# A hybrid convolution and attention block on eight cores: statistics kept per quad, a shorter lead in the output projection, a new order and new first loads

## The chip, the cores and the metric

One Trainium2 chip, eight cores in two dies (cores 0 to 3 and 4 to 7). Each core computes one of eight sequences with the same program and without talking to the others. The metric is the device time of the slowest core, in microseconds. A second, slower state hits some executions of most of these kernels: the cores of one die, sometimes of both, show a lower granted TensorE clock. Only fast runs are compared.

In the views, PE is TensorE (matrix multiplication; PEld are its weight loads), DVE is VectorE, ACT ScalarE, POOL GpSimd, and SP SyncE, which here only issues transfers (DMA). SBUF is the on-chip memory that the program plans by hand; PSUM is the one that matmuls write, used here in eight banks. A table load is an operation that ScalarE's records show between some functions, such as Ln and Silu: 1.28 us each in these traces (mean of 17 on core 2 of the kernel before).

## The reference, cut to what matters

```python
h = rms_norm(x, ln1_g)                         # x: 2048 x 2048 per core
c_val, c_gate, q, k, v = split(h @ w_in)       # 1024 columns each
y = c_val * sigmoid(c_gate)
y = causal_depthwise(y, 31 taps) + b_dw
y_conv = silu(layer_norm over the 1024 channels of y)
y_attn = chunked attention, 8 heads of 128 (band of 9 chunks of 64)
y = concat(rms_norm(y_conv), rms_norm(y_attn))
x = x + y @ w_out                              # called W_out below
h2 = rms_norm(x, ln2_g)
x = x + relu(h2 @ w_ff1)**2 @ w_ff2            # 2048 -> 8192 -> 2048
```

## The kernel before

The program lists its operations once; a scheduler of its own then gives every operation a modelled duration and picks, for each engine, an order that is fixed when the program is built. At run time each engine works through its list and waits where an input is late. So a constant of that model moves instructions without any change to what is computed.

```python
XLAT = 180.0; DMA_LAT = 2200.0; DMA_BPNS = 230.0           # ns, ns, bytes per ns
# GpSimd: 150 + 1.7 n;  DMA issue: 1000 (GpSimd), 60 (SyncE)
# DVE: (n / fast + 130) / .96, transposes as plain copies
```

The tokens are cut into 16 tiles of 128 and four quads of 512; the convolution channels into eight groups. The stages, in order: V (norm of x, transposes, V projection), eight heads of attention, eight conv groups, W_out, feed-forward. The conv groups keep statistics of quad 0 only; those of the other quads are computed inside W_out:

```python
for cc in range(6):                   # groups 0..5
    conv_load(cc + 1)
    for qd in range(4): conv_gate(cc, qd)
    conv_dw(cc)                       # depthwise: 64 small matmuls, all 4 quads
    stat(0, cc, cc == 0)              # Square (ScalarE), ones-matmul, sum on GpSimd
...
for qd in range(4):                   # groups 6 and 7: all gates, then depthwise
    conv_gate(6, qd); conv_gate(7, qd)
for cc in (6, 7):
    conv_dw(cc); stat(0, cc, False)
...
def out_attn(t):                      # attention half of W_out, tile t
    ... 8 transposes of on -> yT ...
    for cb in range(4):
        ... 8 matmuls yT x wo[0] ...
        stt(xx, ps(b), ra[:, t], xx, mult, add)   # VectorE: x += ra * psum
def out_conv(t):                      # conv half, then write out, then the row norm
    ... 4 x (8 matmuls, stt) ...
    P.dma("sp", ..., out_d[t], xs[t % 3])
    norm_tile(...)                    # Square, Ln, Exp (ScalarE), scale (VectorE), 16 transposes
...
fin_stats(0)
for t in range(3): out_attn(t)
for c in range(8): fin_cc(0, c)       # normalise, Silu, Square
fin_end(0)
for t in range(NT):
    out_conv(t)
    if t + 3 < NT:
        loadx2(t + 3)                 # into xs[t % 3], which out_conv(t) has just used
        out_attn(t + 3)
    ... statistics and fin_cc of quad t // 4 + 1 ...
```

Of the kernel before, what the change touches and what calls it, by code (L numbers as in the profile page):

```python
# [22 lines left out]
DMA_LAT = 2200.0  # L23
DMA_BPNS = 230.0
# [22 lines left out]
class Prog:  # L47
# [127 lines left out]
    def _ew(self, eng, fn, r, w, fast=1.0):  # L175
        n = max(self.n(x) for x in w)
        if eng == "dve":
            d = (n / fast + 130) / .96
        else:
            d = 150 + n * 1.7  # L180
        self.op(eng, fn, r, w, d)
# [13 lines left out]
    def ts(self, out, in0, s1, op0, s2=None, op1=None, eng="dve"):  # L195
        r = [in0] + [s for s in (s1, s2) if s is not None and not isinstance(s, float)]
        kw = {} if op1 is None else {"op1": op1}
        self._ew(eng, lambda e: e.tensor_scalar(out=out, in0=in0, scalar1=s1, scalar2=s2, op0=op0, **kw), r, [out])

    def vtr(self, out, in_):  # L200
        self._ew("dve", lambda e: e.transpose(out=out, in_=in_), [in_], [out])
# [10 lines left out]
    def dma(self, eng, key, out, in_, r=(), w=()):  # L212
        r = list(r)
        w = list(w)
        nb = 0
        for x, l in ((in_, r), (out, w)):
            if x.tensor.__class__.__name__.startswith("SB"):
                l.append(x)
                nb = max(nb, self.n(x) * 128 * 4)
        self.op(eng, lambda e: e.dma_start(out=out, in_=in_), r, w, 1000.0 if eng == "pool" else 60.0, dma=True, key=key, nbytes=nb)  # L220
# [167 lines left out]
def build_program():  # L388
# [40 lines left out]
    identf = const("identf", [128], F32)  # L429
    identb = const("identb", [128], BF16)  # L430
    onesf = const("onesf", [128], F32)
    onesb = const("onesb", [128], BF16)
    pv = const("pv", [NPV], F32)
    rk = [const(f"rk{i}", [16], F32) for i in range(2)]
    st1 = const("st1", [16, 2], F32)
    r1 = const("r1", [16], F32)
    st2 = const("st2", [16, 2], F32)
    r2 = const("r2", [16], F32)
    ssa = const("ssa", [16, 8], F32)
    ra = const("ra", [16], F32)  # L440
    rat = const("rat", [16], F32)
    rc = const("rc", [16], F32)
    rct = const("rct", [16], F32)
    rz = const("rz", [16, 1], F32)
    kst = const("kst", [4, 4], F32)
    assert D0 + 53504 <= top[0], (top[0] - D0)
# [18 lines left out]
    P.dma("sp", "id", identf[:, :], id_d)  # L465
# [6 lines left out]

    loadx(0)
    P.dma("sp", "pv", pv[:, :], pv_d)
    P.dma("sp", "g", g1[:, :], bass.AP(gv_d.tensor, 0, [[0, 128], [1, 2048]]))
    for q in range(2):
        P.dma("pool", f"wv0{q}", wv[:, 0, 8 * q:8 * q + 8, :], wv_d[0][:, 8 * q:8 * q + 8, :])
    loadx(1)
    loadx(2)
    for q in range(2):  # L480
        P.dma("pool", f"wv1{q}", wv[:, 1, 8 * q:8 * q + 8, :], wv_d[1][:, 8 * q:8 * q + 8, :])
    copy(identb[:, :], identf[:, :])
# [3 lines left out]
    P.memset(onesf[:, :], 1.0, "dve")  # L486
    P.memset(onesb[:, :], 1.0, "dve")
    P.memset(V[:, :, :, 128:130], 1.0, "pool")
# [16 lines left out]
    for t in range(NT):  # L505
# [6 lines left out]
        norm_tile(xs1[t % 3][:, :], t, st1, r1, g1[:, :], hb[t % 2], dst, (4 + 2 * (t % 2), 5 + 2 * (t % 2)))  # L512
        if t + 3 < NT:
            loadx(t + 3)
        for hf in range(2):
# [10 lines left out]
    EB = [sb(f"EB{i}", [640], BF16, D0 + 1280 * i) for i in range(8)]  # L526
    ef = [sb(f"ef{i}", [256], F32, D0 + 10240 + 1024 * i) for i in range(2)]
    eB = [sb(f"eB{i}", [256], F32, D0 + 12288 + 1024 * i) for i in range(2)]
    gA = sb("gA", [1024], F32, D0 + 14336)
    oj = [sb(f"oj{i}", [128], BF16, D0 + 18432 + 256 * i) for i in range(2)]  # L530
# [3 lines left out]
    def proj(h):  # L534
        hp = h % 2
        for which in (0, 1):
            s = nw[0] % 3
            nw[0] += 1
            P.dma("pool", f"wqk{s}", wqk[s][:, :, :], wqk_d[h, which])
# [71 lines left out]
    P.dma("sp", "g", gA[:, :], bass.AP(gv_d.tensor, 2 * 2048, [[0, 128], [1, 1024]]))  # L611
# [12 lines left out]
    wc = [sb("wc0", [2, 16, 128], BF16, D0 + 24 * KB), sb("wc1", [2, 16, 128], BF16, B + 56 * KB)]  # L624
    pad = sb("pad", [32, 2, 128], BF16, D0)
    raw = sb("raw", [32, 2, 32], BF16, D0 + 16 * KB)
    cs = [sb(f"cs{i}", [512], BF16, D0 + 38 * KB + 8448 + 4096 + 1024 * i) for i in range(2)]
    G = [sb(f"G{i}", [512], BF16, D0 + 32 * KB + 1024 * i) for i in range(2)]
    th = [sb(f"th{i}", [512], F32, D0 + 34 * KB + 2048 * i) for i in range(2)]
    Gt = [sb(f"Gt{i}", [32, 66], BF16, D0 + 38 * KB + 4224 * i) for i in range(2)]  # L630
    ysum = [sb(f"ysum{i}", [512], F32, D0 + 38 * KB + 8448 + 2048 * i) for i in range(2)]
    nv = [0]
    ng = [0]
# [4 lines left out]
    def conv_gate(cc, qd):  # L638
# [4 lines left out]
        bb = []  # L643
        for which in (1, 0):
            b = nv[0] % 3
            nv[0] += 1
            bb.append(b)
            for k in range(16):
                mm(ps(b), w[:, which, k, :], hT[:, qd, k, :], k == 0, k == 15)
            if which == 1:  # L650
                i = ng[0] % 2
                act(th[i][:, :], ps(b), AF.Tanh, scale=0.5)
        stt(G[i][:, :], th[i][:, :], 1.0, ps(bb[1]), ALU.add, ALU.mult)
        ng[0] += 1
        o_ = bass.AP(gt, 1 + 16 * qd, [[32 * 66, 128], [1, 16], [66, 32]])
        P.vtr(o_, G[i][:, :].rearrange("p (b i) -> p b i", i=32))

    def conv_dw(cc):
        s = SLOT[cc]
        gt = Gt[cc % 2]  # L660
        P.dma("pool", "raw", raw[:, :, :, :], toep_d[cc])
        if cc == 0:
            P.memset(pad[:, 0:16, :, :], 0.0)
            P.memset(pad[:, 16:32, :, :], 0.0)
        for ih in range(2):
            for q in range(4):
                P.copy(pad[32 * q:32 * q + 32, 16 * ih:16 * ih + 16, :, 32 * q:32 * q + 32], raw[32 * q:32 * q + 32, 16 * ih:16 * ih + 16, :, :], eng="pool")
        for i in range(32):
            b = 3 + i // 8
            o_ = ps(b, (i % 8) * 64, (i % 8) * 64 + 64)  # L670
            mm(o_, pad[:, i, 0, :], gt[:, i, 1:65], True, False)
            mm(o_, pad[:, i, 1, :], gt[:, i, 0:64], False, True)
        for qd in range(4):
            P.vtr(y[:, s, qd, :].rearrange("p (b i) -> p b i", i=32), bass.AP(psf, 3 * 512 + 16 * qd, [[4096, 128], [1, 16], [64, 32]]))

    def stat(qd, cc, first):
        s = SLOT[cc]
        yy = y[:, s, qd, :]
        su = ysum[qd % 2][:, :]
        if first:  # L680
            P.ts(su, yy, pc(54), ALU.add, eng="pool")
        else:
            tt(su, yy, su, ALU.add, eng="pool")
        c = cs[cc % 2]
        act(c[:, :], yy, AF.Square, scale=0.5, bias=pc(bdw + cc))
        mm(ps(7), onesb[:, :], c[:, :], first, cc == 7)


    h2b = sb("h2b", [2048], BF16, D0 + 32 * KB)
    yT = sb("yT", [8, 128], BF16, D0 + 36 * KB)  # L690
    mu = sb("mu", [512], F32, D0 + 38 * KB)
    rs = sb("rs", [512], F32, D0 + 40 * KB)
    sl = [sb(f"sl{i}", [512], F32, D0 + 42 * KB + 2048 * i) for i in range(2)]

    def fin_stats(qd):
        su = ysum[qd % 2][:, :]
        v2 = sl[0][:, :]

        act(rs[:, :], ps(7), AF.Identity, scale=1.0 / 1024)
        mm(ps(7), onesf[:, :], su, True, True)  # L700
        act(mu[:, :], ps(7), AF.Identity, scale=1.0 / 1024)
        tt(v2, mu[:, :], mu[:, :], ALU.mult)
        stt(rs[:, :], v2, -0.25, rs[:, :], ALU.mult, ALU.add)
# [3 lines left out]
    def fin_cc(qd, cc):  # L707
        s = SLOT[cc]
        yy = y[:, s, qd, :]
        z = sl[cc % 2][:, :]  # L710
        stt(yy, yy, pc(bdw2 + cc), mu[:, :], ALU.add, ALU.subtract)
        tt(yy, yy, rs[:, :], ALU.mult)
        act(z, yy, AF.Silu, scale=pc(lng + cc), bias=pc(lnb + cc))
        P.ts(yb[:, s, qd, 0, :], z, pc(goc + cc), ALU.mult)
        act(yb[:, s, qd, 1, :], z, AF.Square)
        for j in range(4):
            mm(ps(7, j, j + 1), yb[:, s, qd, 1, j * 128:(j + 1) * 128], onesb[:, 0:1], cc == 0 and j == 0, cc == 7, skip=True)

    def fin_end(qd):
        act(rct[:, 4 * qd:4 * qd + 4], ps(7, 0, 4), AF.Ln, scale=1.0 / 1024, bias=pc(epsc))  # L720
        act(rc[:, 4 * qd:4 * qd + 4], rct[:, 4 * qd:4 * qd + 4], AF.Exp, scale=-0.5)

    conv_load(0)
    for cc in range(6):
        conv_load(cc + 1)
        for qd in range(4):
            conv_gate(cc, qd)
        conv_dw(cc)
        stat(0, cc, cc == 0)
    conv_load(7)  # L730
    for qd in range(4):
        conv_gate(6, qd)
        conv_gate(7, qd)
    for cc in (6, 7):
        conv_dw(cc)
        stat(0, cc, False)
# [3 lines left out]
    xo = [D0 + 24 * KB, D0, D0 + 8 * KB]  # L740
    xs = [sb(f"xs{i}", [2048], F32, xo[i]) for i in range(3)]
    g2 = sb("g2", [2048], F32, D0 + 16 * KB)
    for a in (1, 0):
        for cb in range(4):
            P.dma("pool", f"wo{a}{cb}", wo[:, 1 - a, cb, :, :], wo_d[a, cb])
    P.dma("sp", "g", g2[:, :], bass.AP(gv_d.tensor, 2048, [[0, 128], [1, 2048]]))
    pw = [0]

# [3 lines left out]
    def out_attn(t):  # L752
        b = 4
        for k in range(8):
            P.tr(psh[:, b * 1024 + k * 128:b * 1024 + (k + 1) * 128], on[:, t, k * 128:(k + 1) * 128], identb[:, :])
        act(yT[:, :, :], psh[:, b * 1024:(b + 1) * 1024].rearrange("p (k c) -> p k c", c=128), AF.Identity)
        for cb in range(4):
            b = pw[0] % 4
            pw[0] += 1
# [4 lines left out]

    hTb = sb("hTb", [16, 8, 128], BF16, C)

    def out_conv(t):
        qd, ti = divmod(t, 4)
        for cb in range(4):
            b = pw[0] % 4  # L770
            pw[0] += 1
# [13 lines left out]
        norm_tile(xs[t % 3][:, :], t, st2, r2, g2[:, :], h2b, dst, (5, 6))  # L785

    loadx2(0)
# [149 lines left out]
```

## Time and profile before

| | us |
|---|---|
| median of three runs | 2968.6 (2948.3, 2968.6, and 3171.3, slow) |
| profiled run, slowest core (6) | 2975.5 |
| the same run, core 2 | 2946.1 |

The prediction below shows the lines of the page, the dies, the windows and the waits that it rests on. Two views are added here, both of core 2. First, the matmuls of three groups: duration of one in ns (least, median, most), then the start of the first and of the last in us. They give the borders of the stages: V ends with the `wv` row, W_out begins with `yT` (attention half), and its conv half lasts from the first to the last of `yb`.

```profile
L154 PE MATMUL ps<-wv,hT x512: 376/379/634, 31.2 to 179.5; 128*128 128x512 bf16 x171
...
L154 PE MATMUL ps<-wo,yT x512: 379/379/634, 739.9 to 1120.6; 128*128 128x512 bf16 x171
L154 PE MATMUL ps<-wo,yb x512: 379/379/634, 807.1 to 1158.6; 128*128 128x512 bf16 x171
```

Between 739.9, the first attention matmul, and 807.1, the first conv matmul, lie 67.2 us; the conv half then takes 351.5 us. Of W_out's 1024 matmuls of 0.216 us (their spacing at a granted clock of 1.00, taken at 857.17 of the changed kernel in the section on table loads), 96 (three attention tiles) ran before it, so 928 are left, 200 us of work. Second, what VectorE and TensorE waited for in that half (what, what it waited on, us in total, times, longest):

```profile
DVE xs_122 L193 <- DMA xs_122<-x: 33.2, 4, 15.6
...
DVE xs_124 L193 <- DMA xs_124<-x: 22.5, 3, 10.5
...
DVE xs_123 L193 <- DMA xs_123<-x: 16.7, 3, 10.5
...
PE ps L154 <- DVE xs_122 L193: 19.1, 3, 14.6
PE ps L154 <- ACT yb L173: 18.9, 6, 8.9
PE ps L158 <- ACT yT L173: 16.1, 10, 2.4
PE ps L154 <- DVE xs_123 L193: 14.8, 4, 6.6
PE ps L154 <- DVE xs_124 L193: 14.4, 3, 9.7
PE ps L158 <- DVE h2b L193: 3.5, 3, 1.4
```

VectorE waited 72.4 us in ten waits for x tiles, and TensorE 48.3 us behind the additions into those tiles.

### The profile page before, as it was taken

What the parts mean: (1) busy time and instruction counts of PE and PEld (TensorE: products, weight loads), DVE (VectorE), ACT (ScalarE), POOL (GpSimd) and SP (SyncE); (2) the same over time, 40 slices, a digit from 0 to 9 for tenths busy, and PEclk for the clock granted to TensorE, in tenths of its full rate; (3) what the DMA queues carried; (4) which work ended last, traced back from release to release, by engine and by line L of the source; (5) the groups of instructions that cost most, each with busy time, mean ns of one, the idle gap of its engine ahead of it and who ended that gap; (6) DMA issues with size and microseconds to landing.
All of it is one profiled execution on the core that took longest, in us unless ns stands there. A gap on an engine that the chain in (4) does not pass through costs nothing.

```text
span 2975.5 us, 36877 instructions; the slowest of 8 cores (2934.3 to 2975.5 us)
## 1 busy us (share of the span) xinstructions
PE 2774.4 (93%) x13777; PEld 1293.4 (43%) x14048; DVE 915.7 (31%) x1423; ACT 812.0 (27%) x1555; POOL 253.6 (9%) x381
## 2 busy tenths in 40 slices
PE   3999999999477776999999999999999999999999
PEld 1445555444233333444444444444444444444444
DVE  1425655554565333022122122122022122112112
ACT  2427877110455222311211211211211210210210
POOL 0000000543400000000000000000000000000000
PEclk8889999999687788999999999999999999999999
DMA  7321221345413325854444444448854454444424
GB/s 178 128 47 29 33 33 20 50 65 96 103 57 92 98 94 154 173 84 76 81 71 82 74 73 84 71 79 166 210 83 72 76 81 71 81 75 73 83 43 127
DMA packets 112445, 257.81 MB, mean 87 GB/s; under 512 B 5136, under 2 KB 83088, under 8 KB 94480
## 3 DMA queue, kind: packets, MB, share of 16 engines
q0 software_dynamic: 91968, 167.78, 35.0%
q1 hardware_dynamic: 20304, 87.66, 8.8%
q8 instruction: 116, 1.90, 0.3%
q14 instruction: 57, 0.47, 0.1%
HBM read 389.64 MB, written 33.55 MB: 142 GB/s over the span
## 4 chain that ended last, share of the span: by engine, by line
PE 87%; DMA 4%; DVE 3%; ACT 2%; issue 2%; POOL 0%; SPq 0%; DVEq 0%; another core or an unknown queue 0%; ACTq 0%; POOLq 0%
PE ps L154 86%; DMA xa_74<-x 1%; DMA xs_122<-x 1%; DVE h2b L193 1%; DMA w1s_132<-w 1%; PE ps L158 1%; DMA xs_124<-x 1%; DMA xs_123<-x 1%; ACT h2b L173 1%; DVE y L193 0%; DVE y L187 0%; DVE xs_123 L193 0%; ACT cs_105 L173 0%; POOL pad L184 0%; DVE xs_122 L193 0%
## 5 line engine op out<-in xcount | busy, mean ns | idle before, releaser
L187 DVE TENSOR_TENSOR acc<-acc,ps 128x512 f32<-128x512 f32 x512 | 351.8, 688 | 1419.9 <-PE ps L154 1419.9
L154 PE MATMUL ps<-yb,fT 128*128 128x512 bf16 x2688 | 593.9, 379 | 3.4
L154 PEld LDWEIGHTS ps<-yb,fT 128*128 128x128 bf16 x2752 | 269.1, 98 | 325.0 <-issue 1.4
L173 ACT ACTIVATE rl_129<-ps 128x512 f32<-128x512 f32 x128 | 76.5, 598 | 1092.4 <-PE ps L154 1092.3
L154 PE MATMUL ps<-w2s_133,fT 128*128 128x512 bf16 x1314 | 291.1, 379 | 1.6
L154 PE MATMUL ps<-hTb,yb 128*128 128x512 bf16 x1024 | 242.1, 379 | 0.1
L154 PE MATMUL ps<-yb 128*128 128x512 bf16 x989 | 237.9, 379 | 1.8
L154 PEld LDWEIGHTS ps<-w2s_133,fT 128*128 128x128 bf16 x1344 | 131.5, 98 | 158.6
L154 PE MATMUL ps<-wo,yb 128*128 128x512 bf16 x500 | 143.1, 454 | 44.6 <-DVE xs_122 L193 17.2
L220 POOL DMA_DIRECT2D yb<-w x75 | 66.5, 886 | 1278.0 <-PE ps L154 1180.2
L154 PEld LDWEIGHTS ps<-hTb,yb 128*128 128x128 bf16 x1024 | 100.2, 98 | 120.8
L154 PEld LDWEIGHTS ps<-yb 128*128 128x128 bf16 x1024 | 100.2, 98 | 120.3
L173 ACT ACTIVATE rl_130<-ps 128x512 f32<-128x512 f32 x128 | 76.5, 598 | 269.7 <-PE ps L154 269.6
L154 PE MATMUL ps<-wo,yT 128*128 128x512 bf16 x498 | 129.3, 417 | 16.6 <-DVE xs_123 L193 13.0
L154 PE MATMUL ps<-wv,hT 128*128 128x512 bf16 x498 | 132.9, 432 | 1.9 <-issue 0.4
L154 PE MATMUL ps<-yb,w1s_132 128*128 128x512 bf16 x496 | 121.6, 383 | 6.9 <-DMA w1s_132<-w 6.0
L154 PE MATMUL ps<-hTb,w1s_132 128*128 128x512 bf16 x512 | 121.7, 381 | 0.0
L154 PE MATMUL ps<-hTb,w1s_131 128*128 128x512 bf16 x512 | 121.0, 379 | 0.0
L154 PE MATMUL ps<-yb,w1s_131 128*128 128x512 bf16 x496 | 119.6, 379 | 0.8
L154 PE MATMUL ps<-hT,wc_101 128*128 128x512 bf16 x498 | 116.8, 379 | 1.8 <-DVE G_107 L193 1.0
L154 PE MATMUL ps<-hT,wc_102 128*128 128x512 bf16 x498 | 111.7, 379 | 0.7
L154 PEld LDWEIGHTS ps<-wo,yb 128*128 128x128 bf16 x512 | 56.7, 113 | 126.2 <-issue 97.9
(243 smaller groups left out, 2731.1 us busy)
## 6 DMA issues: line engine op xcount, KB each, us to landing
yb<-w POOLq DMA_DIRECT2D x75, 1024.0 KB, 8.8
w2s_133<-w POOLq DMA_DIRECT2D x21, 1024.0 KB, 8.3
acc<-out SPq DMA_DIRECT2D x16, 1024.0 KB, 17.2
w1s_131<-w POOLq DMA_DIRECT2D x16, 1024.0 KB, 8.4
w1s_132<-w POOLq DMA_DIRECT2D x16, 1024.0 KB, 8.3
out<-acc SPq DMA_DIRECT2D x64, 256.0 KB, 5.1
wo<-wo POOLq DMA_DIRECT2D x8, 1024.0 KB, 23.4
xa_72<-x SPq DMA_DIRECT2D x6, 1024.0 KB, 5.7
```

What stands on the lines that cost most here:

```text
L154: self.op("pe", lambda e: e.matmul(out, lhsT=lhsT, rhs=rhs, start=start, stop=stop, skip_group_check=skip), [lhsT, rhs], [out], f * max(n ...
L158: self.op("pe", lambda e: e.transpose(out, in_, ident), [in_, ident], [out], 64.0)
L173: self.op("act", lambda e: e.activation(out=out, in_=in_, func=func, scale=scale, bias=bias, **kw), r, w, d)
L187: self._ew(eng, lambda e: e.tensor_tensor(out=out, in0=in0, in1=in1, op=op), [in0, in1], [out], fast)
L193: self._ew(eng, lambda e: e.scalar_tensor_tensor(out=out, in0=in0, scalar=scalar, in1=in1, op0=op0, op1=op1), r, [out])
L220: self.op(eng, lambda e: e.dma_start(out=out, in_=in_), r, w, 1000.0 if eng == "pool" else 60.0, dma=True, key=key, nbytes=nb)
```

## The change

Its intent: close the holes between the last gate and the feed-forward part, and those of the start. (1) Statistics of all quads are taken in the conv groups; (2) the last two groups run in token halves, and quad 0 is finished between their gates; (3) the attention half of W_out is one tile ahead, not three; (4) an 8 KB gain row spread by matmuls replaces a 1 MB broadcast, and first loads are cut and held back; (5) accumulator loads of the feed-forward part are spread; (6) a new SBUF map; and, with a few lines, (7) new constants of the ordering model. The diff is cut; lines in words stand for longer passages.

```diff
-DMA_LAT = 2200.0
-DMA_BPNS = 230.0
+DMA_LAT = 2000.0
+DMA_BPNS = 310.0
-            d = 150 + n * 1.7
+            d = 100 + n * 1.0
... VectorE transposes 1.2 or 3.6 times as long, one scaling twice as fast;
... DMA issue 900 (GpSimd) and 350 (SyncE) instead of 1000 and 60
+    P.dma("sp", "gr", gr[0:1, :], gv_d[0:1, :])       # 8 KB, then 4 fp32 matmuls
-        for q in range(2): wv0 in halves
+        for q in range(4): wv0 in quarters
+        if t == 1: the second half of V (late) waits for this norm
+        if t == 8: the q/k weights and gA wait for this norm
... conv_dw(cc, q0, nq, bank): for each of its quads
+            act(cs[:, :], yy, AF.Square, scale=0.5, bias=pc(bdw + cc))
+            mm(ps(7)[0:4, :], oh[:, 3 - qd:7 - qd], cs[:, :], ...)
+            tt(ysum[qd], yy, ysum[qd], ALU.add)        # VectorE
... the last two groups
+    for qd in range(2): conv_gate(6, qd); conv_gate(7, qd)
+    conv_dw(6, 0, 2, 3); conv_dw(7, 0, 2, 3); fin_stats(0)
+    for qd in range(2, 4): conv_gate(6, qd); conv_gate(7, qd)
+    for c in range(8): fin_cc(0, c)
+    fin_end(0); out_attn(0); conv_dw(6, 2, 2, 3); out_attn(1); conv_dw(7, 2, 2, 3)
-        if t + 3 < NT: loadx2(t + 3); out_attn(t + 3)
+    seq = [("c", 0), ("f", 1, 0, 4), ("a", 2), ("c", 1), ("f", 1, 4, 8), ("c", 2), ("s", 2), ("a", 3), ...]
-    s1 = [wB(0), wB(2), wD(D0), wD(D0 + 24 * KB)]; s2 = [.., wD(D0 + 8 * KB)]
+    s1 = [wB(0), wB(2), wD(D0 + 8 * KB), wD(D0)];  s2 = [.., wD(D0 + 24 * KB)]
-        for tt_ in range(8): acc_load(tt_)
+                if g == 0: acc_load(2 * jj); acc_load(2 * jj + 1)
```

In `seq`, a is an attention half, c a conv half, f normalisation steps of a quad, s its statistics.

## The prediction

> **What bounds the kernel now.** I read the page first (busy shares and the 40 slices), then the table of cores and dies, then a table of windows with one row for each stage of core 2, then the chain that ended last, and last the timeline inside the projection stage.
>
> ```profile
> span 2975.5 us, 36877 instructions; the slowest of 8 cores (2934.3 to 2975.5 us)
> ...
> PE 2774.4 (93%) x13777; PEld 1293.4 (43%) x14048; DVE 915.7 (31%) x1423; ACT 812.0 (27%) x1555; POOL 253.6 (9%) x381
> ...
> PE   3999999999477776999999999999999999999999
> ...
> PEclk8889999999687788999999999999999999999999
> DMA  7321221345413325854444444448854454444424
> ```
>
> TensorE is the bound over the whole, but slices 1 and 11 to 16 show holes, and the granted clock dips in the same slices. Slice 17 on is the feed-forward part: full.
>
> ```profile
> die 0 (median of its cores): 2941.5 us, clock 0.968
> die 1 (median of its cores): 2969.4 us, clock 0.955
> ```
>
> The dies differ by 28 us. Core 6 (die 1) had 0.83 in its V stage and 0.81 in its W_out stage, core 2 (die 0) 0.96 and 0.86. I therefore count on core 2 and add the clock at the end. Its stages, columns: window, its length, busy time of PE, weight load, DVE, ACT, POOL, then clock, DMA share, GB/s:
>
> ```profile
> 0.00:50.30 50.30, 10.85 (x61) 6.08 (x62) 11.03 (x14) 8.78 (x13) 4.34 (x12) 0.90 0.96 209
> 502.00:724.00 222.00, 216.33 (x1385) 104.31 (x1382) 114.31 (x92) 26.63 (x45) 96.56 (x96) 1.00 0.44 76
> 724.00:807.50 83.50, 46.47 (x263) 21.66 (x264) 50.09 (x62) 38.01 (x54) 33.24 (x25) 0.64 0.34 77
> 807.50:1158.00 350.50, 258.75 (x1336) 117.93 (x1335) 149.79 (x189) 127.03 (x176) 3.30 (x4) 0.86 0.35 104
> 1158.00:1230.00 72.00, 62.71 (x306) 28.86 (x305) 4.35 (x4) 23.59 (x38) 4.28 (x6) 0.93 0.90 184
> 1230.00:2946.00 1716.00, 1710.38 (x7925) 774.89 (x7923) 351.32 (x512) 296.45 (x483) 87.64 (x118) 1.00 0.49 87
> ```
>
> The start is bound by transfers (DMA 0.96, PE busy 11 of 50). Conv is bound by TensorE. The two stages from 724 to 1158, 434 us, are bound by waits: first conv's last statistics, then W_out. The feed-forward row loses 6 us of 1716, so the change can win little there. Inside the hole, the chain (core 6: start, length, what):
>
> ```profile
> 751.64 1.04 POOL pad L184
> ...
> 765.61 1.75 DVE rs L193
> 767.36 2.97 DVE y L193 x2
> ...
> 774.14 1.28 ACT L173
> ...
> 800.76 0.73 ACT cs_105 L173
> ```
>
> With the gates done, the chain runs through pad copies, transposes, squares, mean, variance, normalisation, then quad 1's squares; TensorE has nothing independent queued. And inside W_out (core 2, timeline):
>
> ```profile
> 957.27 1.05 PE L158 MATMUL ps<-identb,h2b 128*128 128x128 bf16 x16 [1.26 <-DVE h2b L193]
> 962.63 2.73 DVE L193 SCALAR_TENSOR_TENSOR xs_124<-ps,ra,xs_124 128x512 f32<-128x512 f32 x4 [5.50 <-DMA xs_124<-x]
> 963.53 9.36 PE L154 MATMUL ps<-wo,yb 128*128 128x512 bf16 x32 [1.87 <-DVE xs_124 L193]
> ```
>
> The attention half of tile t+3 adds into the buffer that tile t has just left. Write-out and reload of 1 MB sit in front of that add, four PSUM banks stay full, TensorE waits, and its next 32 matmuls take 9.36 us instead of 6.9.
>
> [...] the same VectorE operation takes 0.75 us alone and 1.75 us at 765.61, beside a GpSimd sum. [...]
>
> **The change part by part.** Unit: a full-clock 128x512 matmul every 0.2158 us (32 take 6.9 us).
>
> *Start.* In 50.3 us the old kernel moves all V weights, four x tiles, a 1 MB broadcast gain and three q/k weights, and has issued only 16 V matmuls. The change sends an 8 KB gain row (spread by a matmul), puts the first half of V in front, and holds the second half until x tile 4 has landed and q/k until tile 8. What is needed for the first halves comes sooner, but the bytes before the second half of V (six x tiles, all V) nearly equal the old total, and the small gain row queues behind the parameters, which took 13.3 us to land. So I expect the first V matmul at 20 to 28 us (was 31), and at 51 us about 80 to 96 V matmuls done rather than 16: 70 x 0.2158 = 15 us won.
>
> *Conv.* Per group, four squares go through one buffer and four 4-row matmuls, plus four adds on VectorE instead of one on GpSimd. Square, matmul, square takes 0.72 + 0.58 + handovers = 1.5 us, while the instruction order gives five gate matmuls and the statistic (1.3 us) between: 0.2 x 4 x 8 groups = 6 us lost. VectorE rises to some 19 of 33 us a group: no bound.
>
> *Last groups and W_out.* TensorE's work from 724 to 1158: 1024 matmuls 221 us, 384 transposes at 66 ns 25, small and statistic ones 21, together 267; so 434 - 267 = 167 us are lost. The change adds 128 depthwise matmuls at 33 ns and four fp32 selections, some 8 us. What loss stays: (a) quad 0: its chain is transposes 1.7, square and statistic 1.8, mean 2.4 + 0.7, variance 1.7, loads and Ln/Exp 2.9, normalise 0.8, load, Silu, Square 2.8: 15 us, against 61 gate matmuls (13.2 us) placed before its first use; then 8 steps at 1.9 us on VectorE covered by two attention tiles: about 8 us lost. (b) The conv half of W_out, 4 MB, can only start after the gates of quads 2 and 3, and competes with 3 x tiles and a broadcast: about 5. (c) One tile of lead frees an x buffer two tiles (some 30 us) before its next add, where write and load need 5 + 8: this wait goes. (d) The norm chain of a tile (6.4 us, from the same timeline on core 6) is covered by 32 matmuls, 6.9 us; with one table load it is not. The new ScalarE order alternates between Silu and Ln/Exp 26 times (the old 19 times, where the trace has 17 loads); three tiles have a Silu wedged between a tile's Ln and Exp, three loads on that chain: 5 us each; six others 3 us: about 33. Sum lost 46 to 50. Stage: 267 + 8 + 50 = 325, won 109.
>
> *Feed-forward.* Its first 72 us lose 9 to contention of 8 MB of accumulator loads with the weights; they are now issued two per weight tile: 8 won.
>
> Sum on an undisturbed die: 15 - 6 + 109 + 8 = 126 us.
>
> **The clock.** On die 1 the old W_out stage ran at 0.77 to 0.79 for about 200 us, and waits hid that. A denser stage shows it: 200 x 0.19 = 38 us, less what remained visible, 30. There I expect 96 us.
>
> **The rivals.** First, ScalarE becomes the bound of W_out: 5.7 us of tile work, 4.3 of three normalisation steps and 2.6 to 5 of loads make 12.6 to 15 of a 15.1 us tile. For it: three engines near full in fixed orders. Against: its share in that stage is 127 of 350 now. If so, nine tiles take 20 us each: 2890. Second, the new single buffers in conv (gate banks 0 and 1, one G, one square) stall TensorE each quad: 32 x 1.4 us would give back 45 us, 2895. Against: a transposed G needs 3.2 us in a period of 6.9. Third, the gaps close nearly fully, because the fixed order now has work for every hole: loss 20 instead of 50, 2800. Fourth, all is hidden by the clock [...]: 2900.
>
> **Range and chances.** Old fast runs were 2948 to 2977, the median 2968.6. 2948 - 126 = 2822 where no die throttles, 2970 - 96 = 2874 where one does; I predict 2850. Eight in ten: 2795 to 2900. Two per cent is 59 us (2909), below which all but a conjunction of rivals stay: faster 0.91, within 0.07, slower 0.02.
>
> **What would show it.** Right: windows of W_out with PE busy over 90% and no wait of VectorE on x loads; the hole after the last gate gone; V matmuls counted at 51 us over 70; table loads near 24, with TensorE waiting for the normalised tile in the middle tiles only; feed-forward unchanged. Wrong: in conv, TensorE waiting on squares or G for over 15 us; the first V matmul later than 31 us; an x wait in W_out; or W_out lasting over 340 us on die 0.

## The result, and the profile after

The changed kernel ran in 2791.7, 2789.8 and 2791.3 us (fast) and once in 2967.2 (slow: die 0 at 0.92); the kernel before, in the same rounds, in 2948.3, 2968.6 and 2947.4 (fast) and 3171.3 (slow). The ratio is 0.9446 (95% interval 0.9384 to 0.9507): faster by 5.5%. A ratio is the mean time of one kernel's fast runs over the mean of the other's fast runs of the same rounds, so not quite the ratio of the medians that are quoted. The prediction, 2850 with a range of 2795 to 2900, was 58.5 us too slow, and the result lies just below the range.

The page and the dies, now (core 5 was the slowest):

```profile
span 2790.2 us, 37523 instructions; the slowest of 8 cores (2783.8 to 2790.2 us)
...
PE 2727.9 (98%) x14192; PEld 1271.9 (46%) x14192; DVE 930.0 (33%) x1460; ACT 822.6 (29%) x1561; POOL 227.9 (8%) x367
...
PE   6999999999989999999999999999999999999999
...
PEclk9999999999999999999999999999999999999999
...
die 0 (median of its cores): 2786.0 us, clock 0.995
die 1 (median of its cores): 2786.6 us, clock 0.995
```

The hole of slices 11 to 16 and the dips of the clock are gone, and both dies agree. Core 2, windows (columns as before: window, length, busy PE, weight load, VectorE, ScalarE, GpSimd, clock, DMA share, GB/s):

```profile
0.00:50.30 50.30, 29.03 (x120) 14.24 (x120) 19.34 (x23) 15.20 (x24) 4.42 (x12) 0.97 0.91 204
...
724.50:748.60 24.10, 21.25 (x175) 10.36 (x176) 20.32 (x28) 12.18 (x18) 9.93 (x9) 0.93 0.56 114
748.60:1011.00 262.40, 243.19 (x1446) 118.96 (x1445) 167.38 (x216) 141.00 (x187) 7.80 (x9) 0.98 0.46 140
1011.00:2787.40 1776.40, 1769.72 (x8209) 801.64 (x8207) 354.88 (x514) 318.90 (x518) 91.68 (x123) 1.00 0.51 93
```

The start has 29 us of TensorE work instead of 11, the old hole before the conv half 21 in 24, the conv half of W_out 243 in 262. The borders of the stages and TensorE's waits from the last gates on:

```profile
L154 PE MATMUL ps<-wv,hT x512: 376/379/634, 20.7 to 163.0; 128*128 128x512 bf16 x171
...
L154 PE MATMUL ps<-wo,yT x512: 376/379/634, 724.5 to 1003.0; 128*128 128x512 bf16 x171
L154 PE MATMUL ps<-wo,yb x512: 376/379/634, 748.6 to 1010.8; 128*128 128x512 bf16 x171
...
PE ps L158 <- DVE h2b L193: 13.9, 4, 4.1
PE ps L154 <- DVE xs_124 L193: 2.0, 1, 2.0
PE ps L154 <- ACT yb L173: 1.7, 3, 1.3
```

Read against the rows of before: V's last matmul starts at 163.0 instead of 179.5; from there to the first attention matmul 561.5 us (before 560.4); from there to the first conv matmul 24.1 (67.2); the conv half 262.2 (351.5); from there to the end of core 2's span 1776.6 (1787.5). The gain of core 2, 2946.1 - 2787.4 = 158.7 us, is 16.5 - 1.1 + 43.1 + 89.3 + 10.9. One attention tile has changed sides in this: 96 attention matmuls ran before the first conv matmul, now 64, so 6.9 of the 43.1 us are work that moved into the conv half. TensorE's waits, of which the largest are shown, add up to 24 us, 13.9 of them for the normalised tile `h2b`; of waits for x transfers VectorE has one left, of 0.2 us.

### The profile page after: what moved, and what is told of

It reads as the page before. It is cut to its first block, busy times and chain, and to the rows that moved or that the text cites. A ratio compares the mean times of both kernels' runs of the same rounds, so it can differ in the third digit from the quotient of the medians.

```text
span 2790.2 us, 37523 instructions; the slowest of 8 cores (2783.8 to 2790.2 us)
## 1 busy us (share of the span) xinstructions
PE 2727.9 (98%) x14192; PEld 1271.9 (46%) x14192; DVE 930.0 (33%) x1460; ACT 822.6 (29%) x1561; POOL 227.9 (8%) x367
## 4 chain that ended last, share of the span: by engine, by line
PE 93%; DVE 2%; ACT 2%; issue 2%; DMA 1%; POOL 0%; SPq 0%; DVEq 0%; ACTq 0%; POOLq 0%
PE ps L154 91%; PE ps L158 1%; DMA xa_73<-x 1%; DVE Gt_110 L201 0%; DVE h2b L193 0%; DMA eB_94<-relb 0%; DVE Gt_109 L201 0%; DVE G L193 0%; ACT L173 0%; DVE y L193 0%; DVE y L201 0%; DVE hb_75 L193 0%; POOL pad L184 0%; ACT cs L173 0%; ACT hb_75 L173 0%
## 5 line engine op out<-in xcount | busy, mean ns | idle before, releaser
L154 PE MATMUL ps<-wo,yT 128*128 128x512 bf16 x512 | 119.0, 386 | 1.4 <-ACT yT L173 0.9
L154 PE MATMUL ps<-hT,wc_101 128*128 128x512 bf16 x512 | 119.6, 379 | 0.0
L154 PE MATMUL ps<-wo,yb 128*128 128x512 bf16 x512 | 118.5, 389 | 0.0
L154 PE MATMUL ps<-wv,hT 128*128 128x512 bf16 x512 | 116.5, 389 | 0.4 <-DVE hT L184 0.2
L154 PE MATMUL ps<-hT,wc_102 128*128 128x512 bf16 x512 | 116.1, 379 | 0.9 <-DMA wc_102<-wcg 0.9
L154 PE MATMUL ps<-hT,wqk_66 128*128 128x512 bf16 x384 | 97.1, 379 | 0.0
```

Of the source, the lines that this page charges most:

```text
L154: self.op("pe", lambda e: e.matmul(out, lhsT=lhsT, rhs=rhs, start=start, stop=stop, skip_group_check=skip), [lhsT, rhs], [out], f * max(n ...
```

## The experiments

Eighteen runs, all with correct results, on four chips; undisturbed runs of the kernel before take 2949 to 2953 us on each of them. This table gives for twelve of them (the other six are in the text) the median of the fast runs and, for core 2 unless noted, the five lengths read as above from the same three rows: V's last matmul, from there to the first attention matmul, to the first conv matmul, the conv half, the rest.

| kernel | fast median | V | to attention | to conv | conv half | rest |
|---|---|---|---|---|---|---|
| before | 2948.3 (later 2950 to 2952) | 179.5 | 560.4 | 67.2 | 351.5 | 1787.5 |
| changed | 2791.3 | 163.0 | 561.5 | 24.1 | 262.2 | 1776.6 |
| u_lead | 2884.8 | 161.0 | 562.0 | 43.1 | 346.1 | 1774.1 |
| u_model | 2817.1 | 165.7 | 574.1 | 39.0 | 252.2 | 1780.7 |
| u_early | 2811.0 | 161.3 | 580.9 | 30.8 | 254.8 | 1775.7 |
| u_start | 2802.9 | 174.6 | 561.4 | 24.1 | 262.0 | 1776.5 |
| u_stat | 2795.7 | 161.8 | 553.7 | 25.0 | 274.6 | 1775.7 |
| banks3 | 2788.6 | 159.4 | 560.9 | 24.6 | 258.5 | 1775.6 |
| b_lead | 2859.0 | 178.8 | 560.4 | 55.7 | 260.5 | 1791.1 |
| b_model | 2901.3 (one) | 171.4 | 559.5 | 30.7 | 349.9 | 1776.0 |
| b_two (core 5) | 2857.7 | 170.7 | 559.1 | 22.4 | 284.2 | 1783.2 |
| b_four | 2811.8 | 157.0 | 560.9 | 23.6 | 285.2 | 1776.3 |
| tab2 | 2809.3 | 163.6 | 564.4 | 24.4 | 277.1 | 1780.0 |
| best2 | 2786.0 | 159.5 | 561.7 | 24.1 | 256.5 | 1775.6 |

V's end moves by up to 4 us between runs of the same start (159.4 to 163.6), so differences of that size in a single profile are not read.

### The lead

u_lead: the changed kernel with three tiles of lead again.

```diff
+    seq = [it for it in seq if it[0] != "a"]
+    ... ("a", 2) first, then ("a", t + 3) directly behind ("c", t)
```

> The new kernel with the attention half of tile t+3 again put right after the conv half of tile t, into the x buffer just left. Theory of the x wait: VectorE waits on x transfers about 10 times for some 70 us in W_out and TensorE behind it loses 40 to 50 us, as in the kernel before (72.4 us in 10 waits, 48 us behind them); with lost clock +40 to +60 us. Rival: in the new order other work (quad steps) fills TensorE and the one-tile lead is worth under 15 us.

Measured: 2884.8 us, 93.5 more, well above the 40 to 60 expected. The waits of VectorE on x transfers and of TensorE behind it, in W_out:

```profile
DVE xs L193 <- DMA xs<-x: 63.6, 10, 12.3
...
PE ps L154 <- DVE xs L193: 42.3, 12, 9.8
PE ps L158 <- ACT yT L173: 18.1, 10, 2.3
PE ps L154 <- ACT jk L173: 12.2, 9, 3.5
```

Ten waits on x transfers are back, as in the kernel before, and 42 us of TensorE behind them as expected; 30 us more are waits on `yT` and `jk` (1.1 and 2.4 in the changed kernel), which the expectation left out, and the clock from 748.6 to 1011 fell to 0.84. The rival (the order fills the gaps) falls: nothing filled them.

b_lead: the kernel before, with the shorter lead alone.

```diff
-    for t in range(3): out_attn(t)
+    for t in range(2): out_attn(t)
-            loadx2(t + 3); out_attn(t + 3)
+            loadx2(t + 3)
+        if t + 2 < NT: out_attn(t + 2)
```

> The kernel before with one part of the change alone: two attention tiles ahead at first and the attention half of tile t+2 (not t+3) after the conv half of tile t. Undoing the lead in the new kernel had cost 96 us. If the lead is worth that by itself, this kernel gains 60 to 100 us on the one before (ratio 0.966 to 0.98) and the waits of VectorE on x transfers (72 us in 10 waits) fall under 15 us. If it is worth it only together with statistics kept per quad and an early quad 0 (which give TensorE other work and free ScalarE), it gains 15 to 40 us and other waits (on the normalised tile, yT, statistics) take the place of the x wait.

Measured: ratio 0.9677 (0.958 to 0.9775), fast runs 2856.3, 2859.0 and 2876.9 (the last with part of die 1 at 0.97).

```profile
L154 PE MATMUL ps<-wo,yb x512: 376/379/631, 794.9 to 1055.4; 128*128 128x512 bf16 x171
...
PE ps L154 <- DMA w1s<-w: 13.3, 1, 13.3
```

The conv half takes 260.5 us, as in the changed kernel (262.2), and VectorE has no wait on x transfers in it. So three lines of the change, without statistics per quad or an early quad 0, give the whole gain of that stage: 91.0 us, where the changed kernel has 89.3. What does not come with them is the hole before it (55.7) and the start of the feed-forward part, where a wait of 13.3 us for a weight tile is seen.

### The constants of the ordering model

u_model: the changed kernel with the old constants.

```diff
-DMA_LAT = 2000.0; DMA_BPNS = 310.0
+DMA_LAT = 2200.0; DMA_BPNS = 230.0
... and the old durations of GpSimd, VectorE transposes and DMA issues
```

> The new kernel ordered with the old constants of the ordering model (slower transfers and GpSimd, faster VectorE transposes, cheap issues); the program is the same, only the fixed order of each engine differs. If the constants matter, +10 us or more, most in the conv and W_out stages; the prediction gave them nothing, which means within 5 us.

Measured: 2817.1 us, 25.8 more: 12.6 before the first attention matmul, 14.9 before the first conv matmul, 4 at the end, less 10 in the conv half; the 2.7 at the start are within what V's end moves. b_model: the kernel before with the new constants alone (the same lines the other way).

> The kernel before with the new constants of the ordering model alone. In the new program undoing them cost 26.5 us. If they are worth that by themselves, ratio 0.991 or 25 us faster; if they only help a program that has free work to choose from (here the x wait sets W_out), within 10 us of the kernel before.

Measured: one fast run, 2901.3 us, 50 less than the kernel before (2951.4); in the three slow runs the dies that were not disturbed (two of them) lay at 2892 to 2909.

```profile
L154 PE MATMUL ps<-wo,yb x499: 376/379/634, 761.6 to 1111.5; 128*128 128x512 bf16 x167
L154 PE MATMUL ps<-wo,yT x497: 376/379/634, 730.9 to 1077.5; 128*128 128x512 bf16 x166
...
PE ps L154 <- DVE xs L193: 34.7, 8, 10.3
```

The hole before the first conv matmul shrinks from 67.2 to 30.7 us, V ends 8 us sooner, and the wait at the start of the feed-forward part is gone too; the conv half stays at 349.9, with the additions still behind x transfers. The rival (constants only help where there is free work) falls: the work was there, in the wrong order.

b_two: both, in the kernel before; b_four: b_two with the new first loads and the spread accumulator loads, still without (1), (2) and (6).

> The kernel before with the shorter lead and the new ordering constants, nothing else. If the lead works on W_out (91 us in the trace of that run) and the constants on the hole before it (45 us in the trace of theirs), they add: 2951 - 97 - 50 = 2804, ratio 0.95. If they share their gain, 2840 or more.

> The same with the new first loads and the spread accumulator loads as well: no statistics per quad, no token halves, no early finish of quad 0. From the runs so far 2804 - 11.5 (loads) - 10 (accumulators) = 2783, as fast as the new kernel, which would mean that its restructured conv adds nothing to these four. If the restructuring closes what the constants leave of the hole, this stays 15 to 25 us behind the new kernel, 2805 to 2815.

Measured: b_two 2857.7 us, ratio 0.9686 (0.967 to 0.9702), no better than b_lead in this number. The profile shows a disturbed die beside an undisturbed one; V's window on core 2 (die 0, `171` is V's end) and core 5 (die 1):

```profile
50.30:171.00 120.70, 112.96 (x567) 54.66 (x576) 45.42 (x37) 47.97 (x80) 0.82 (x3) 0.83 0.41 125
...
50.30:171.00 120.70, 114.17 (x680) 58.13 (x678) 48.06 (x41) 49.91 (x84) 0.83 (x3) 0.97 0.40 124
807.50:1030.00 222.50, 195.07 (x1143) 95.07 (x1142) 127.75 (x163) 121.87 (x165) 3.30 (x4) 0.98 0.45 138
```

The clock in V is 0.83 on one die and 0.97 on the other, whose cores ended at 2820 to 2827, about 120 us below the undisturbed cores of the kernel before (2934 to 2950). In three of the four fast runs both dies had the lower mean clock (0.977 to 0.981), so its median is not that of an undisturbed kernel. So of 93 + 50, the two gains by themselves, about 120 come together: the edits work on different stages (22.4 before the first conv matmul, where the constants had left 30.7), but the conv half rises from 260.5 to 284.2 us. In it core 5 has 16.3 us of waits for `h2b` (b_lead 8.3) and 14.7 for `yT` (b_lead 14.0). Why that order is worse there was not tried. b_four: 2811.8 us, ratio 0.9542 (0.952 to 0.9564), 20 us behind the changed kernel. That is the second branch of its expectation: the restructured conv with its own order is worth some 20 us, and they lie in the conv half (285.2 against 262.2).

### Quad 0, the statistics, the first loads

u_early: all gates of groups 6 and 7 first, then their depthwise, then quad 0, as before.

```diff
-    conv_dw(6, 0, 2, 3); conv_dw(7, 0, 2, 3); fin_stats(0)      # between the gates
+    ... all gates ...; conv_dw(6, 0, 4, 3); conv_dw(7, 0, 4, 3); fin_stats(0)
```

The scratch tiles of quad 0 move too, since their old places are then still in use.

> The new kernel with all gates of groups 6 and 7, then their whole depthwise, then quad 0's finish, as the kernel before had it. Theory: the hole after the last gate comes back; in the kernel before the row 724 to 807.5 had 46.5 us of TensorE work in 83.5, of which 13 us waited for the first x sums; now with one yT ahead and statistics kept per quad I expect a hole of 20 to 30 us[...]: +25 to +35 us. Rival: the statistics kept per quad are what closed the hole, and the early finish is worth under 10 us.

Measured: 2811.0 us, 19.7 more, between the two. The loss is 19.4 us before the first attention matmul and 6.7 behind it, with 9.6 us of waits for pad copies and a granted clock of 0.56 from 720.6 to 748.6 us; the conv half gains 7 back.

u_stat: squares, statistic matmuls and sums of quads 1 to 3 back in W_out; banks3 is its control.

```diff
             act(cs[:, :], yy, AF.Square, ...)    # in the conv groups: quad 0 alone
+        if qd:                                   # in fin_stats(qd)
+            for c in range(8): stat(qd, c)
-        w = (0, 1, 5, 7) if t > 1 else (0, 1, 5)     # this line in both
+        w = (0, 1, 5)
```

> The new kernel with the squares, statistic matmuls and sums of quads 1 to 3 moved back out of the conv groups to just before each quad's mean in W_out (24 squares, 24 matmuls, 24 adds), with output banks 0, 1, 5 for all tiles. Against its control with those banks alone. Theory: some 2.5 us of ScalarE and VectorE work each for 24 steps falls into W_out where ScalarE has some slack: +10 to +25 us over the control. Rival: conv pays now what W_out would pay then (conv gets 6 us shorter) or the order fills it: within 5 us of the control.

> The control for the run with the statistics moved back: the new kernel with W_out's output banks 0, 1, 5 in turn for all tiles instead of 0, 1, 5, 7. Three banks still leave two groups of matmuls (3.4 us) for VectorE's add of 0.7 us: under +4 us. If VectorE is often late by more than that, +10 or more.

Measured: 2795.7 and 2788.6 us, so 7 us for the statistics, where the first theory expected 10 to 25. The table shows why: conv gets 7.2 us shorter and the conv half of W_out 16.1 longer. The prediction's "6 us lost" in conv is about right, and it is bought with more. Three banks cost nothing.

u_start: the changed kernel with the old first loads.

```diff
-    ... gain row, 4 fp32 matmuls, copies; wv0 in quarters; late, mark
+    P.dma("sp", "gr", g1[:, :], bcast(0, 2048)); wv0 in halves; nothing held back
```

> The new kernel with the old first loads (1 MB broadcast gain, first V half in two pieces, nothing held back). Theory: the start is bound by transfers and whatever comes before the V stage ends is passed on in full, so the V stage ends near 179 us instead of 163 and the time rises by 15 to 17 us. Rival: the later stages run by deadlines of their own (transfers of weights) and swallow a part: +5 or less.

Measured: 2802.9 us, 11.5 more, and V ends 11.6 us later: all is passed on, as the theory says, but the loads are worth 11.5 us, not 15 to 17. The other 5 of the 16.5 us at the start came with something else: the constants alone, with the old loads, moved V's end by 8.

### The feed-forward part

u_acc: the eight accumulator loads at once; u_map: the old places of two weight buffers; u_accmap: both.

```diff
-                if g == 0: acc_load(2 * jj); acc_load(2 * jj + 1)     # u_acc, u_accmap
+        for tt_ in range(8): acc_load(tt_)
-    s1 = [.., wD(D0 + 8 * KB), wD(D0)];  s2 = [.., wD(D0 + 24 * KB)]   # u_map, u_accmap
+    s1 = [.., wD(D0 + 8 * KB), wD(D0 + 24 * KB)];  s2 = [.., wD(D0)]
```

> The new kernel with the eight 1 MB accumulator loads issued at once at the start of each half of the feed-forward part. Theory: the first 72 us of that part lose 9 us to contention with the weights as in the kernel before, so +8 to +11 us. Rival: the contention came from weights whose buffers are freed late, not from the accumulators: under 3 us.

> The new kernel with the old places of two feed-forward weight buffers: the fourth first-layer buffer lies where x tile 15 was (the last to leave), the third second-layer buffer where tile 14 was. Issuing the accumulator loads at once cost nothing, so the 9.3 us wait of the kernel before, which was for that weight tile, must come from its place or from the other transfers at that time. Theory of the place: the wait comes back, +7 to +10 us. Rival: in the new kernel the stage ends with fewer transfers pending, so the tile lands in time anyway: under 3 us.

> The new kernel with both the old accumulator loads (eight at once) and the old places of the two weight buffers. Theory: each of the two suffices to hide the wait, so that both undone bring it back: TensorE waits 9 to 13 us for a first-layer weight tile at the start of the feed-forward part (9.3 us in the kernel before, 13.3 in that kernel with the shorter lead), +9 to +13 us. Rival: the shorter lead and the earlier W_out loads removed it, and both undone cost under 3 us.

Measured: u_acc 2789.9 us and u_map 2790.5 and 2791.6 (a third run, 2831.0, had die 0 at 0.978 to 0.989): nothing. u_accmap 2801.6: 10 us. Core 1 of it:

```profile
PE ps L154 <- DMA w1s<-w: 8.4, 1, 8.4
```

Each of the two parts hides the wait by itself, so undoing one shows nothing, and the prediction's attribution (accumulator loads alone) would have passed for right or been called worthless by a single run.

### The table loads

tab2: a needless Silu between Ln and Exp in six tiles that had none.

```diff
         act(st[:, t, 1:2], st[:, t, 0:1], AF.Ln, scale=1.0 / D, bias=pc(epsc))
+        if sw and t >= 10: act(st[:, t, 0:1], st[:, t, 1:2], AF.Silu)   # sum already used
```

> The new kernel with a needless Silu of one column between Ln and Exp of the norm in tiles 10 to 15, which had no Silu there: two more table loads of 1.28 us and one small instruction, about 2.9 us more on each of six norm chains. The prediction's reckoning (a chain of 6.4 us under 6.9 us of matmuls, so 0.5 us of slack) makes it +14 us. If TensorE has more than that to do before it needs the normalised tile, which the smaller losses in the trace suggest, less: about +4 us or nothing.

Measured: 2809.3 us, 18 more, 3.0 a tile: even more than the prediction's own reckoning. First the changed kernel, TensorE's four waits for the normalised tile (start, length, what, idle time before it; behind the first of them also the matmuls that follow), and then two of tab2's:

```profile
818.14 1.30 PE L158 MATMUL ps<-identb,h2b 128*128 128x128 bf16 x16 [4.00 <-DVE h2b L193]
819.23 8.12 PE L154 MATMUL ps<-wo,yb 128*128 128x512 bf16 x30
...
838.66 1.33 PE L158 MATMUL ps<-identb,h2b 128*128 128x128 bf16 x16 [4.06 <-DVE h2b L193]
...
890.62 1.05 PE L158 MATMUL ps<-identb,h2b 128*128 128x128 bf16 x16 [1.79 <-DVE h2b L193]
...
910.23 1.24 PE L158 MATMUL ps<-identb,h2b 128*128 128x128 bf16 x16 [4.01 <-DVE h2b L193]
```

```profile
948.64 1.65 PE L158 MATMUL ps<-identb,h2b 128*128 128x128 bf16 x16 [2.18 <-DVE h2b L193]
...
967.79 1.05 PE L158 MATMUL ps<-identb,h2b 128*128 128x128 bf16 x16 [2.18 <-DVE h2b L193]
```

An idle time of 2.18 us stands before these tiles' transposes, where the prediction's arithmetic (2 loads less 0.5 us of slack) says 2.1, and after it some transposes are slower (1.65 us in the first line, 1.05 in the second). All six waits of tab2 add up to 13.5 us; the rest of the 18 lies in such slower work and in smaller shifts. So the price of a load on this chain was right. The same holds for the changed kernel's three waits of 4 us: behind the first, 30 matmuls take 8.12 us (granted clock 0.82), where 32, each with its own weights, take 7.07 at a clock of 1.00 (at 857.17; the last of them takes 0.38, so they follow each other at (7.07 - 0.38) / 31 = 0.216 us), and with such slowing each of the three costs some 5.8 us. What failed was the count. ScalarE of the changed kernel at the wait of 818.14:

```profile
809.59 0.19 ACT L173 ACTIVATION_READ_ACCUMULATOR h2b<-xs_124 128x1 f32 x1
809.68 0.62 ACT L173 ACTIVATE jk_122<-sl_120 128x512 bf16<-128x512 f32 x1
810.30 1.28 ACT L173 ACT_TABLE_LOAD   x1
811.60 0.30 ACT L173 ACTIVATE st<-st,pv 128x1 f32<-128x1 f32 x1
811.91 1.28 ACT L173 ACT_TABLE_LOAD   x1
813.21 0.82 ACT L173 ACTIVATE sl_119<-y,pv 128x512 f32<-128x512 f32 x1
814.04 1.28 ACT L173 ACT_TABLE_LOAD   x1
815.34 0.20 ACT L173 ACTIVATE rn<-st 128x1 f32<-128x1 f32 x1
```

Sum, load, Ln, load, Silu, load, Exp: three loads and a Silu on the chain, and a wait of 4.0 us of TensorE. The loads cost their own 1.28 us and little more: the next instruction starts 0.02 us after the first one's end (811.60), and in tab2 two added loads with a small Silu lengthen ScalarE's way from the start of Ln to the start of Exp from 0.39 us (938.86 to 939.25 in the changed kernel) to 3.24 (942.60 to 945.84), by 2.85 us. Three tiles are like this one, as the prediction counted from the order. Of the other six of its list two had a load on the chain (one waited 1.79 us, at 890.62, the other nothing); the other four had none: the last load on record before their Ln and Exp is that of a quad's own Ln (1.28 us at 786.62, for `rct`) or one of an earlier tile's norm (1.28 us at 834.57, for the Ln at 851.78).

adj: Exp is made to follow Ln at once, everywhere; best: adj, with the second half of V held back to x tile 5; best2: the order fix in W_out alone, with banks3.

```diff
         act(r[:, t:t + 1], st[:, t, 1:2], AF.Exp, scale=-0.5)
+        P.ops[-1].prio = -1              # best2: only for the norms of W_out
-                    lat = 60.0           # in the model, same engine
+                    lat = 0.0 if so.prio < 0 else 60.0
-        if t == 1:                       # best
+        if t == 5:
```

> The new kernel with one change of its order: the Exp of a row norm directly follows its Ln on ScalarE, so no Silu (and no pair of table loads) comes between. Table theory: three tiles of W_out lose two loads of 1.28 us and a Silu of 0.8 from their chain, 3.4 us each, and since the run with needless switches showed no slack in that chain (18 us for six tiles), TensorE gains 9 to 12 us, its wait for the normalised tile falls from 13.9 us to under 5, and the time to about 2780. Rival: those waits merely hide VectorE's or ScalarE's other work, which then is waited for: under 4 us.

> Meant to beat both kernels: Exp directly behind Ln as in the other run, and the second half of the V weights (4 MB) held back until x tile 5 is normalised instead of x tile 1. In the new kernel 48 V matmuls were issued by 51 us and TensorE idled some 40 us of the first 50. With the first half of V alone, a tile needs 5 us of transfer and 4.5 us of TensorE, so TensorE should be busy from about 25 us and the V stage end 6 to 12 us sooner, near 153 us instead of 163. With the 9 to 12 us of the order, 2768 to 2776. Rival for the start: the model issues second-half matmuls before the weights land and TensorE waits for them in its fixed order; then nothing or a loss.

> Meant to beat both: Exp directly behind Ln in W_out alone, output banks 0, 1, 5 for all tiles, the start as in the new kernel. By the trace the order fix gained 6.5 us in W_out (279.8 us from first to last of its matmuls, 286.3 without it). If that stands alone, 2781 to 2785; if the table loads only hide other waits, 2788 as the banks alone.

Measured: adj 2789.9 us, within 2 us of the changed kernel, so the table theory's 9 to 12 us did not come. The triple loads are gone, but the waits for `h2b` fall only from 13.9 us in 4 to 9.5 in 7; the stage from first attention to last conv matmul is 279.8 instead of 286.3 us, and V and conv, whose order changed too, lose 4 (2.6 of them at V's end, within what it moves). Why waits for `h2b` remain is open. best: 2800.1, a loss:

```profile
PE ps L158 <- DVE hb L193: 17.0, 7, 3.6
...
PE ps L154 <- DMA wv<-wv: 2.5, 2, 2.2
```

Norms of x tiles came too slowly for a TensorE that had only half of V to do (17 us of waits against 13 in the changed kernel), and then the weights came late: V ended at 170.1. The step from tile 1 to tile 5 was too far. best2: 2785.0 to 2787.2 in four fast runs, ratio 0.9441 (0.9427 to 0.9454), about 5 us below the changed kernel (two more runs were slow). That misses the first branch of its expectation: banks3 alone is at 2788.6, so the order fix is worth some 2.6 us of the 5, not the 6.5 that adj's trace showed in W_out.

after2: the changed kernel once more, as a control for such differences.

> The changed kernel itself, unchanged, as the control for the small differences. If its first three fast runs hold in another call, 2789 to 2793; if they move by more than 3 us, the differences below 7 us of the other runs are not to be trusted.

Measured: 2791.1, 2791.4 and 2791.9 us in three fast runs (three more were slow). So best2's fast runs lie wholly below those of the changed kernel, which makes it the fastest version found, by 0.2%; the two were run neither in the same call nor on the same chip.

## Why the prediction was right or wrong

Faster by over 2% was right, and so was the order of the stages that gain. Two steps failed: the clock term, and the residual loss of W_out. The time was 58.5 us too high, in two parts: 28 of the clock (2850 - 2822) and 30.5 of the sum (126 us predicted for an undisturbed core, 158.7 measured on core 2, less 2 to 3 us by which the base of 2948 was low).

**The clock: wrong.** The step "A denser stage shows it ... There I expect 96 us" put 2850 halfway between 2822 and 2874. It took one disturbed die of one profile (0.955 against 0.968) for a property of the kernel. Later, eight of nine runs of the kernel before had both dies at 0.966 to 0.970 and 2949 to 2953 us, and all six fast runs of the changed kernel had every core at 0.993 to 0.996. Its denser W_out runs at 0.98 on core 2 in the table of windows, where the old one had 0.86, and its feed-forward part, 1772 us of dense matmuls (1011 to 2783), at 1.00 on all eight cores. A part-disturbed run does occur (2831 in u_map, 2976 among the runs of the kernel before, most runs of b_two), but as a state of some executions. What brings it about stays open. The base should have been the undisturbed 2951.

**The last groups and W_out: right in mechanism, mis-sized.** Predicted, with conv: 109 - 6 = 103 us; measured 43.1 + 89.3 - 1.1 = 131.3. The term that failed is the residual loss "46 to 50", measured 24 in waits and some 5 in which work behind the three long waits ran slow. In it (d) "about 33" for the norm chains was 19: the three tiles cost some 5.8 us each, where 5 was said, but of the "six others 3 us" one cost 1.8 and five nothing. (b) "about 5" for the second half of the weights was 0. (a) "about 8" for quad 0 stands against the remaining 10 us of waits, of several kinds. The residue of some 7 us lies in the conv term: 6 lost and 8 of added work were expected, and the way to the first attention matmul grew by only 1.1, though the statistics cost it 7 (u_stat). It was not taken apart further.

**(c), the x wait: right**, and much the largest part: 93.5 us undone, and 93 alone (2859.0 against 2952.2). The prediction said that the wait goes, but gave it no share of its own. More buffers were not needed for it: there are three x buffers before and after, and the shorter lead alone removed the wait (b_lead).

**The constants: missed.** The diff's first lines got no number, though the order of every engine hangs on them. They were worth 50 us alone and 26 undone. The hole that (a) ascribes to quad 0's early finish is closed in part by either: 36.5 us of it by the constants in the old program. Undone one by one, the parts come to 93.5 + 25.8 + 19.7 + 11.5 + 10.3 + 7.1 = 168 of some 160 us: some 8 us need two parts at once and are counted twice.

**The start: right in size by accident.** 15 us predicted, 16.5 measured. But by 50.3 us 48 V matmuls were started, not 80 to 96; the gain row landed at 7.9 us and not late, and the rest was won after 50 us. Of the 16.5, the loads are 11.5.

**The feed-forward part: right in size (8, measured 10.9), half right in cause.** The spread accumulator loads suffice, and so does the new place of the weight tile.

**The rivals.** ScalarE as the bound (2890) and stalls in conv (2895) did not come: 141 us of 262 busy, and 6 us of conv waits in all. The third, that the gaps close nearly fully (20 lost, 2800), is what happened; it had been left at the edge of the range. Its sum was off as well: 30 us less loss gives 2822 - 30 = 2792 without the clock term, or 2850 - 30 = 2820 with it, but not 2800.

## What to carry to other kernels

Read the clock of several runs before a disturbed die goes into a prediction: one profile cannot tell a kernel's property from a state of the chip (die 1 at 0.955 in the one profile here, both dies at 0.966 to 0.970 in eight of nine later runs). Where instructions are ordered by a model when the program is built, a changed constant of the model is a change of the kernel, and it should be undone by itself like any other part. And undo parts in pairs as well as one by one: two parts that each hide the same wait look worthless singly.
